# Moving low parts and differences of activation forms from VectorE to GpSimd in a one-layer decoder step

## The chip, the cores and the metric

The kernel runs on one core of a Trainium2 chip. In the profile the core's engines are PE (TensorE matmul), PEld (its weight load), DVE (VectorE), ACT (ScalarE), POOL (GpSimd) and SP (SyncE, here only a queue of transfers). The metric is the device time of one execution in microseconds (us). It is the median of three runs: 2129.26 us, with 2129.08 and 2132.24 as the lowest and the highest.

## The reference

One inference step of a hybrid decoder layer, in float32, for 512 prompt tokens and 8 sample tokens (so 520 columns of activations when features lie on the partitions):

```python
def trunk(x, ...):                       # DEPTH = 1, D_MODEL = 2048, D_FF = 5632
    m, c_new, s_new = mixer(rmsnorm(x, norm_mix_g), ...)
    x = x + m
    f, f_new = conv_ffn(rmsnorm(x, norm_ffn_g), ...)
    x = x + f
    return rmsnorm(x, final_norm_g), ...

def mixer(xn, ...):
    bg, cg, hin, q, k, v, og, glr = split(xn @ w_in, ...)       # 2048 x 6160
    ya = bg * causal_dwconv(cg * hin, conv_prev, conv_w)        # 1024 channels
    o, s_new = gla_chunked(q, k, v, logf, s0)                   # 4 heads
    yb = rmsnorm_per_head(o) * silu(og)
    return concatenate([ya, yb]) @ w_out, ...                   # 2048 x 2048

def conv_ffn(xn, ...):
    u, v = split(xn @ w_up, 2)                                  # 2048 x 11264
    return (silu(causal_dwconv(u, ...) + conv_b) * v) @ w_down  # 5632 x 2048
```

The outputs are the two sets of activations and the new convolution and recurrence states.

## The kernel before

**Number form.** Every float32 operand of a large product is held as two fp32r tiles, a high part `hi` (a rounding copy, made by ACT) and a low part `lo` = source - `hi` (made by DVE). A product is three matmul passes: high weights by high activations, low by high, high by low. For activations the function `split` makes the pair: line 123 is ACT's copy, line 124 is DVE's subtraction. For weights it is `prepare`: line 1381 (ACT) and line 1385 (DVE), on tiles of 128x1024.

**Seven products in place of eight.** From the second part of the input projection on, the products are done in a seven-product block scheme: the activations of a block row are combined into seven *forms* (numbers 1 to 7; 1, 2 and 3 are plain quarters, 4 to 7 are differences and sums), the weights into seven sums, and `ORDER = (1, 5, 6, 2, 7, 3, 4)` is the order in which the seven products are run. The table `INPUT = {1: 1, 2: 2, 3: 3, 4: 7, 5: 5, 6: 4, 7: 6}` says which form product r reads. Each product is 24 matmuls of 260 columns. A form exists for four groups of feature rows (g = 0 to 3), each a pair of 128x520 tiles.

**Stages.** Input projection with the recurrence; the *mixer* (12 sets of seven products, the rest of the input projection); the output projection (`wo`, two chunks of four groups, seven products each); the up projection of the ConvFFN (44 sets of seven); the down projection; the final norm. A loop over all products (the order's step i) emits, for each step, the matmuls, the evacuations of the step before (`mix_finish`, `chunk_finish` with DVE line 1670, `up_finish`), the parts of the weights for step i + 2 (`prepare`), and small steps of generators that say at which offset from their start they want to go on (`yield 7.5`). The program order that results is kept as it stands on PE, DVE, ACT, POOL and SP: each of them works strictly in that order.

**Where the output projection ends.** In its second chunk, the results of group g are complete after the group. The generator `projected(g)` (line 1693) then stores them (`x1_d`, SP), scales the four quarters into temporaries `xg[0..3]` (ACT, line 1707), makes the squares for the norm (ACT, added into `ssq` and `R` by POOL transfers, line 1717) and builds the forms of the up projection: forms 1, 2, 3 by `split`; t1, t2, t3, t4 by DVE (lines 702 and 696) for forms 5, 4, 6 and 7. Form 7 and, for the last group, all forms are split at once; t1, t2, t3 of the groups 0 to 2 go to memory (`t_d`, SP) and come back with `load_sum` in the last group, where `split_sums` splits them, each at a fixed offset. The up projection's first products read all of this. Forms 2 and 3 are written into the tiles of finished sums (`acc`), so that the writer must wait until the transfer to `x1_d` has read those.

**Where the mixer begins.** `load_sum(mt_d, f, g)` loads forms 5, 4, 6 and 7 of the layer's input, which were put in memory earlier; the lists `put[:3]`, `put[3:6]` and the generator `put_sums` split them at fixed places. Two of them (form 7, groups 0 and 1) use `split_by_dma`: ACT writes the high part and its negative, and a POOL transfer adds the source to that.

**Temporaries** come from a pool of eight 128x520 tiles that are used in turn.

Of the kernel before, what the change touches and what calls it, by code (L numbers as in the profile page):

```python
# [9 lines left out]
F32 = mybir.dt.float32  # L10
F32R = mybir.dt.float32r
U8 = mybir.dt.uint8
AF = mybir.ActivationFunctionType
ALU = mybir.AluOpType
# [8 lines left out]
T = NP + NS  # L23
# [14 lines left out]
def trunk_kernel(  # L38
# [6 lines left out]
    nc = tc.nc  # L45
# [46 lines left out]
    def tmp():  # L92
        return tp.tile([P, T], F32, tag="t", name="t")

    def two(ap):
        return ap.rearrange("p (a b) -> p a b", a=2)
# [24 lines left out]
    def split(src, hi, lo, scale=None):  # L121
        if scale is None:
            nc.scalar.activation(hi, src, AF.Copy)  # L123
            nc.vector.tensor_tensor(lo, src, hi.bitcast(F32), op=ALU.subtract)  # L124
        else:
            nc.scalar.activation(hi, src, AF.Copy, scale=scale)
            nc.vector.scalar_tensor_tensor(
                lo, src, scale, hi.bitcast(F32), op0=ALU.mult, op1=ALU.subtract
            )

    def split_by_dma(src, hi, lo, again=None):
        nc.scalar.activation(hi, src, AF.Copy)
        nc.scalar.activation(lo, hi.bitcast(F32), AF.Copy, scale=-1.0)
        again = src if again is None else again
        nc.gpsimd.dma_start(lo.bitcast(F32), again, accum_op=ALU.add)

    def halves(t):
        return t[:, :HT], t[:, HT:T]
# [115 lines left out]
    def moving(pool, tag, name):  # L254

        return pool.tile([P, T + 3], F32R, tag=tag, name=name)[:, 3:]

    def pair_tiles(pool, tag):

        return [  # L260
            moving(pool, f"{tag[0]}{s}{tag[1:]}", tag[0] + s) for s in "hl"
        ]
# [17 lines left out]
    t_d = dp.tile([3, 3, P, T], F32, name="t_d")  # L280
    mt_d = dp.tile([4, 4, P, T], F32, name="mt_d")
# [55 lines left out]
    with ExitStack() as es:  # L337
# [208 lines left out]
        for k in range(KD):  # L546
            c, t = k // 4, k % 4
# [147 lines left out]
    def minus(out, ps, x):  # L695
        nc.vector.scalar_tensor_tensor(out, ps, -1.0, x, op0=ALU.mult, op1=ALU.subtract)

    def add(out, x, y):
        nc.vector.tensor_tensor(out, x, y, op=ALU.add)  # L699

    def sub(out, x, y):
        nc.vector.tensor_tensor(out, x, y, op=ALU.subtract)
# [42 lines left out]
    def acc_tag(n):  # L745
        return f"x{'hl'[n % 2]}{8 + n // 2}"
# [5 lines left out]
    def form(f, g):  # L752

        if f == 1:
            x = pair_tiles(bigA, f"b{g}")
        elif f in (2, 3):
            x = [
                moving(bigA, acc_tag(4 * g + q), "b2")
                for q in ((0, 3) if f == 2 else (1, 2))
            ]  # L760
        else:
            k = homes.get((f, g), {5: 0, 4: 4, 6: 8, 7: 12}[f] + g)
            x = [moving(slots[k], f"y{s}{k}", f"y{s}{k}") for s in "hl"]
        for j, q in enumerate(zip(*(halves(y) for y in x))):
            xq[f, 2 * g + j] = q
        return x

    def first_tile(kind, g, m):

        return 4 * g + 2 * m if kind == "down" else 2 * g + 8 * m  # L770

    def rows_of(d, kind, g, q):

        m, b = first_tile(kind, g, q // 2), q % 2
        return d[m : m + 2, :, b * HT : (b + 1) * HT].rearrange("m p c -> p m c")
# [45 lines left out]
    def mix_source(n, m, k):  # L821
        what, j = MIX[n]
        c0 = {"ch": 1024 * m + j * P, "b": (j + m - 1) * P, "og": 5120 + (j + m - 1) * P}[what]
        return w_in[(k - 1) * 1024 : k * 1024, c0 : c0 + P].rearrange("(k p) c -> p k c", p=P)

    def second_half(source):

        raw = {}
        for k in (1, 2):
            w = raw[2, k] = wxr.tile([P, 1024], F32, tag="raw", name="raw")  # L830
            src = source(2, k)
            nc.sync.dma_start(w.rearrange("p (k c) -> p k c", k=src.shape[1]), src)
        return raw
# [11 lines left out]
    with ExitStack() as mix:  # L845
# [46 lines left out]
        with ExitStack() as gl:  # L892
# [9 lines left out]
            for j in range(4):  # L902
                nc.gpsimd.affine_select(
                    out=sel, in_=sel, compare_op=ALU.not_equal, fill=1.0,
# [340 lines left out]
            for h in range(NH):  # L1245
# [21 lines left out]
                for d in range(2):  # L1267
                    ps = group(h > 0 and d == 0)
                    t = gp.tile([P, T], F32, tag="v", name="v", bufs=2)
# [16 lines left out]
    NG = KD // 4  # L1286
# [19 lines left out]
    def raw_tile(source, k):  # L1306

        w, src = wp.tile([P, 1024], F32, tag="raw", name="raw"), source(1, k)
        return w, (w.rearrange("p (k c) -> p k c", k=src.shape[1]), src)
# [285 lines left out]
    def fh():  # L1595
        return wxp.tile([P, T], F32, tag="fh", name="fh")
# [94 lines left out]
    ssq, loaded = [], deque()  # L1691

    def projected(g):

        xg = {}

        def ready(q):
            a, m = acc[g, q], first_tile("wo", g, q // 2)
            kept = a
            if g == NG - 1 and q in (1, 2):  # L1700

                kept = tmp()[:, :T]
                nc.scalar.activation(kept, a, AF.Copy)
            nc.sync.dma_start(rows_of(x1_d, "wo", g, q), two(kept))
            xg[q] = tmp()[:, :T]
            for j in range(2):
                nc.scalar.activation(
                    halves(xg[q])[j], halves(a)[j], AF.Copy, scale=gffn[:, m + j : m + j + 1]
                )

        def square(q):
            if g == 0 and q in (0, 3):
                nc.scalar.activation(ssq[q % 2], acc[g, q], AF.Square)
                return
            sq = fh()
            nc.scalar.activation(sq, acc[g, q], AF.Square)
            nc.gpsimd.dma_start(ssq[q % 2], sq, accum_op=ALU.add)

        def out(f, t):

            if f == 7 or g == NG - 1:
                split(t, *form(f, g))
            else:
                nc.sync.dma_start(t_d[f - 4, g], t)

        yield 4.5
        ready(0)
        split(xg[0], *form(1, g))
        yield 5.5
        ready(3)  # L1730
        square(0)
        yield 6.5
        ready(1)
        square(3)
        yield 7
        t1, t2 = xg[0], tmp()[:, :T]
        sub(t1, xg[0], xg[1])
        minus(t2, t1, xg[3])
        yield 7.5
        ready(2)  # L1740
        out(5, t1)
        yield 8
        split(xg[2], *form(2, g))
        t4 = xg[2]
        minus(t4, t2, xg[2])
        yield 8.5
        out(4, t2)
        yield 9
        square(1)
        out(7, t4)  # L1750
        yield 10
        t3 = xg[1]
        sub(t3, xg[3], xg[1])
        yield 10.5
        square(2)
        out(6, t3)
        yield 11
        split(xg[3], *form(3, g))

    def load_sum(d, f, g, by_dma=False):  # L1760

        hi, lo = form(f, g)
        x = lo.bitcast(F32)
        nc.sync.dma_start(x, d[f - 4, g])
        if by_dma:
            return lambda: split_by_dma(x, hi, lo, d[f - 4, g])
        return lambda: split(x, hi, lo)

    def split_sums():

# [36 lines left out]
    wxr = yctx.enter_context(tc.tile_pool(name="raw2", bufs=4, side="right"))  # L1807
    wxp = yctx.enter_context(tc.tile_pool(name="sums", bufs=2, side="right"))
    early = second_half(lambda m, k: mix_source(0, m, k))
    put = [load_sum(mt_d, 5, g) for g in range(1, 4)]  # L1810
    early[1, 1], first = raw_tile(lambda m, k: mix_source(0, m, k), 1)
    nc.sync.dma_start(*first)
    ps = new_mm()
# [8 lines left out]
    assert not side  # L1822
    begin(0)
    load_rest(0)
    put += [load_sum(mt_d, 4, g) for g in range(1, 4)]
    on = [tmp()[:, :T] for _ in range(2)]
    for j, x in enumerate(on):
        nc.sync.dma_start(x, o_d[j])
    put += [load_sum(mt_d, 6, g) for g in range(1, 4)]
    y8, y9 = zpad[0][:, 2 : 2 + T], tmp()[:, :T]  # L1830
    evac(ps, y8)
    nc.scalar.activation(y8, y8, AF.Silu)
# [16 lines left out]
    bctx.close()  # L1849
    yt3 = yctx.enter_context(tc.tile_pool(name="yt3", bufs=1))  # L1850
    slots[12:] = [yt3] * 4
    put += [load_sum(mt_d, 7, g, g < 2) for g in range(4)]
    for k in range(8):
        for f, kk, b in ((1, k, 0), (2, k + 8, 0), (3, k + 8, 1)):
            xq[f, k] = [xa[kk][x][b] for x in range(2)]
# [7 lines left out]
        yield from leave(8, y8, y9)  # L1863

    def put_sums():
        for x, n in zip(put[6:], (1, 1.5, 2, 2.5, 3, 4, 4.5)):
            yield n
            x()

# [2 lines left out]
    for i, (kind, at, r) in enumerate(order):  # L1872
        j, n = i % 7, i // 7
# [41 lines left out]
        if i in (0, 2, NW, NW + 2):  # L1915

            x = xq[1, 0][0]
# [14 lines left out]
        if kind == "wo":  # L1932
            c, g = at
            if c == 0 and g == 2 and j == 0:
                load_form("wo", 1, 0)
            if c == 0 and j == 4 and g + 1 < NG:
                load_residual(g + 1)
            if c == 0 and g == 2 and j == 1:
                add_residual("wo", 0)
            if c == 0 and g == NG - 1 and j >= 1:  # L1940
                load_form("wo", 1, j)
            if c == 1 and g == NG - 1:

                for f, h in {
                    0: ((5, 0), (5, 1)), 2: ((5, 2),), 3: ((4, 0), (4, 1)), 4: ((4, 2),),
                    5: ((6, 0), (6, 1)), 6: ((6, 2),),
                }.get(j, ()):
                    loaded.append(load_sum(t_d, f, h))
        if 7 * n in (NM - 7, NU - 7):
            for x in {1: (0, 1), 2: (2, 3), 4: (4, 5), 6: (6,)}.get(j, ()):  # L1950
                load_form(groups[n + 1][0], 0, x)
# [2 lines left out]
        if kind == "down":  # L1954
            c, g = at
# [166 lines left out]
```

## Time and profile before

| What | Value |
|---|---|
| median of three runs | 2129.26 us |
| the profiled execution, its own time | 2130.32 us |
| span in its trace | 2128.6 us |
| PE busy | 2106.9 us (99%) |
| DVE busy | 1763.2 us (83%) |
| ACT busy | 1125.9 us (53%) |
| POOL busy | 421.0 us (20%) |
| granted TensorE clock, mean | 0.998 |

The profile lists, for each engine, when an instruction began, how long it took, and in square brackets how long the engine had been idle and what ended that. `x3` after a row means three like instructions in a row that are shown as one. Matmuls overlap: 24 matmuls of 260 columns are one product and follow each other in 2.86 us. DVE instructions overlap a little too: the start-to-start distance is smaller than the duration shown. "PE mm" and "PE ms" are products of the mixer and the up projection, "PE x", "y", "e" and "f" those of the output and the down projection, by the names of the accumulators.

### The profile page before, as it was taken

The page shows a single profiled execution, that of the slowest core. Times are in us where ns is not written, and L with a number is a line of the kernel's source. Part 1 is how long each engine was busy: PE and PEld are TensorE (multiplying, and loading weights), DVE is VectorE, ACT ScalarE, POOL GpSimd, SP SyncE. Part 2 cuts the span into 40 slices and gives each one's busy share as a digit, 9 for nine tenths or more (in the row PEclk, how much of TensorE's full clock was granted, in tenths as well). Part 3 has the DMA queues.
Part 4 walks back from the last instruction along what each step waited for, and adds up shares of the span by engine and source line. Part 5 has one row for each costly group of instructions (what it writes and reads, how often), then busy time and mean ns, then how long its engine had stood idle before and what let it go on. Part 6 is the DMA issues. An engine that isn't in the chain of part 4 may idle for free.

```text
span 2128.6 us, 44249 instructions
## 1 busy us (share of the span) xinstructions
PE 2106.9 (99%) x17880; PEld 2086.8 (98%) x17880; DVE 1763.2 (83%) x2355; ACT 1125.9 (53%) x1701; POOL 421.0 (20%) x614
## 2 busy tenths in 40 slices
PE   9999999999999989999999999999999999999997
PEld 8999999999999989999999999999999999999997
DVE  6566675988888998989889989989989778888886
ACT  7454554655544776555555555555555554444445
POOL 4211221121235211211311221212212200300000
PEclk9999999999999999999999999999999999999999
DMA  8456546877789995766766766766767876994734
GB/s 258 131 169 185 164 137 186 236 199 200 192 263 278 269 287 133 196 175 171 195 177 167 196 176 167 196 176 168 195 176 193 282 227 153 274 295 131 220 110 160
DMA packets 468190, 418.37 MB, mean 197 GB/s; under 512 B 21817, under 2 KB 426569, under 8 KB 467841
## 3 DMA queue, kind: packets, MB, share of 16 engines
q1 hardware_dynamic: 424209, 289.84, 48.0%
q0 software_dynamic: 43728, 125.63, 22.6%
q8 instruction: 140, 2.29, 0.5%
q14 instruction: 65, 0.53, 0.1%
q10 hardware_dynamic: 48, 0.07, 0.0%
HBM read 300.18 MB, written 80.31 MB: 179 GB/s over the span
## 4 chain that ended last, share of the span: by engine, by line
PE 93%; DVE 2%; DMA 2%; ACT 1%; issue 1%; POOL 0%; SPq 0%; ACTq 0%; DVEq 0%; POOLq 0%
PE mm L1408 37%; PE ms L1408 15%; PE mm L146 12%; PE x L1651 9%; PE y L1651 9%; PE e L1651 4%; PE f L1651 4%; DMA raw<-in_w_in_dram 1%; DMA wgraw<-in_w_in_dram 1%; PE ms L1071 0%; DMA yl<-t_d 0%; DVE yl L124 0%; DMA t_d<-t 0%; PE ms L2012 0%; PE tp L365 0%
## 5 line engine op out<-in xcount | busy, mean ns | idle before, releaser
L1408 PE MATMUL mm<-yh,hi 128*128 128x260 f32 x1792 | 500.8, 281 | 2.5 <-DVE t L699 1.3
L1408 PE MATMUL mm<-yl,hi 128*128 128x260 f32 x1792 | 498.9, 281 | 2.5 <-DVE yl L124 2.5
L1408 PE MATMUL mm<-yh,lo 128*128 128x260 f32 x1792 | 496.4, 280 | 0.0
L1381 ACT ACTIVATE hi<-raw 128x1024 fp32r<-128x1024 f32 x336 | 354.4, 1055 | 243.4 <-issue 89.0
L1385 DVE TENSOR_TENSOR lo<-raw,hi 128x1024 fp32r<-128x1024 f32 x336 | 410.3, 1221 | 45.3 <-ACT hi L1381 41.4
L1385 DVE TENSOR_TENSOR lo<-s,hi 128x1024 fp32r<-128x1024 f32 x252 | 309.3, 1228 | 132.7 <-ACT hi L1381 132.7
L1381 ACT ACTIVATE hi<-s 128x1024 fp32r<-128x1024 f32 x252 | 266.3, 1057 | 227.5 <-PE ms L1408 97.3
L1408 PEld LDWEIGHTS mm<-yh,hi 128*128 128x128 f32 x1792 | 337.7, 188 | 3.6 <-issue 1.5
L1408 PEld LDWEIGHTS mm<-yl,hi 128*128 128x128 f32 x1792 | 335.0, 188 | 3.3 <-DVE yl L124 3.3
L1408 PEld LDWEIGHTS mm<-yh,lo 128*128 128x128 f32 x1792 | 335.9, 189 | 0.0
L1408 PE MATMUL ms<-b,hi 128*128 128x260 f32 x1408 | 264.9, 280 | 0.0
L1408 PEld LDWEIGHTS ms<-b,hi 128*128 128x128 f32 x1408 | 222.0, 188 | 0.0
L1651 PE MATMUL y<-form,hi 128*128 128x260 f32 x1120 | 211.5, 281 | 0.8 <-DVE acc L1670 0.8
L1651 PE MATMUL x<-form,hi 128*128 128x260 f32 x1120 | 211.6, 281 | 0.0
L1326 DVE TENSOR_TENSOR s<-s,raw 128x1024 f32<-128x1024 f32 x168 | 205.3, 1222 | 2.9
L1408 PE MATMUL ms<-b,lo 128*128 128x260 f32 x704 | 196.4, 280 | 0.0
L1651 PEld LDWEIGHTS y<-form,hi 128*128 128x128 f32 x1120 | 176.5, 188 | 1.2 <-ACT yh L123 1.0
L1651 PEld LDWEIGHTS x<-form,hi 128*128 128x128 f32 x1120 | 176.5, 188 | 0.2
L1651 PE MATMUL x<-form,lo 128*128 128x260 f32 x560 | 156.9, 280 | 0.0
L1651 PE MATMUL y<-form,lo 128*128 128x260 f32 x560 | 156.8, 280 | 0.0
L1408 PEld LDWEIGHTS ms<-b,lo 128*128 128x128 f32 x704 | 132.0, 187 | 0.0
L1408 PE MATMUL mm<-bh,hi 128*128 128x260 f32 x448 | 124.9, 280 | 1.0 <-DVE acc L1670 1.0
(405 smaller groups left out, 4825.2 us busy)
## 6 DMA issues: line engine op xcount, KB each, us to landing
raw<-in_w_up_dram SPq DMA_DIRECT2D x176, 512.0 KB, 4.0
raw<-in_w_down_dram SPq DMA_DIRECT2D x96, 512.0 KB, 7.3
raw<-in_w_in_dram SPq DMA_DIRECT2D x92, 512.0 KB, 4.1
form<-f_d SPq DMA_DIRECT2D x126, 260.0 KB, 6.3
raw<-raw POOLq DMA_DIRECT2D x60, 512.0 KB, 5.8
f_d<-t POOLq DMA_DIRECT2D x80, 260.0 KB, 5.5
raw<-in_w_out_dram SPq DMA_DIRECT2D x32, 512.0 KB, 12.5
form<-g_d POOLq DMA_DIRECT2D x42, 260.0 KB, 7.5
```

The lines of the kernel that those rows point to most:

```text
L146: nc.tensor.matmul(o, w, xx, start=first and i == 0, stop=last and i == 2)
L1326: return lambda: nc.vector.tensor_tensor(out, x, y, op=ALU.add)
L1381: nc.scalar.activation(his[i], src, AF.Copy)
L1385: nc.vector.tensor_tensor(los[i], src, his[i].bitcast(F32), op=ALU.subtract)
L1408: nc.tensor.matmul(st["bank"][b], w[:, k, :], x, start=b not in st["used"] and (k, j) == (0, 0), stop=(k, j) == (7, 2), skip_group_check=True,
L1651: nc.tensor.matmul(ps[:, m, :], w[:, k, m * P : (m + 1) * P], x, start=b not in st["used"] and k == 0 and j == 0, stop=k == 3 and j == 2, ...
```

## The change

`split_by_pool` takes the place of `split_by_dma`: ACT makes the high part as before, and the low part is made by a GpSimd subtraction. It is used

- in `projected(g)` for groups 0 to 2 in forms 1, 2 and 3, and for all four groups in form 7;
- in `split_sums` for four of the nine loaded sums: form 5 of groups 0 and 1, form 4 of group 0, form 6 of group 0;
- where the mixer begins for forms 5, 4 and 6 of group 1 and form 7 of groups 0 and 2; form 7 of group 1 becomes a plain `split` (DVE), and two of the offsets of `put_sums` move by half a step.

The difference t3 of groups 0 to 2 goes to GpSimd as well (`psub`). In `projected(g)` form 2 is made 1.5 steps later (offset 9.5, behind forms 4 and 7) for all groups, and t4 gets a temporary of its own instead of being written over `xg[2]`.

```diff
-    def split_by_dma(src, hi, lo, again=None):
+    def split_by_pool(src, hi, lo):
         nc.scalar.activation(hi, src, AF.Copy)
-        nc.scalar.activation(lo, hi.bitcast(F32), AF.Copy, scale=-1.0)
-        again = src if again is None else again
-        nc.gpsimd.dma_start(lo.bitcast(F32), again, accum_op=ALU.add)
+        nc.gpsimd.tensor_tensor(lo, src, hi.bitcast(F32), op=ALU.subtract)
...
+    def psub(out, x, y):
+        nc.gpsimd.tensor_tensor(out, x, y, op=ALU.subtract)
...
     def projected(g):
-        xg = {}
+        xg, final = {}, g == NG - 1
+        some = split if final else split_by_pool
...
         def out(f, t):
-            if f == 7 or g == NG - 1:
+            if f == 7:
+                split_by_pool(t, *form(f, g))
+            elif final:
                 split(t, *form(f, g))
             else:
                 nc.sync.dma_start(t_d[f - 4, g], t)
...
-        split(xg[0], *form(1, g))
+        some(xg[0], *form(1, g))
...
         yield 8
-        split(xg[2], *form(2, g))
-        t4 = xg[2]
+        t4 = tmp()[:, :T]
         minus(t4, t2, xg[2])
...
         out(7, t4)
+        yield 9.5
+        some(xg[2], *form(2, g))
         yield 10
         t3 = xg[1]
-        sub(t3, xg[3], xg[1])
+        (sub if final else psub)(t3, xg[3], xg[1])
...
-        split(xg[3], *form(3, g))
+        some(xg[3], *form(3, g))
...
-    put = [load_sum(mt_d, 5, g) for g in range(1, 4)]
+    put = [load_sum(mt_d, 5, g, g == 1) for g in range(1, 4)]
...
-    put += [load_sum(mt_d, 7, g, g < 2) for g in range(4)]
+    put += [load_sum(mt_d, 7, g, g % 2 == 0) for g in range(4)]
...
-        for x, n in zip(put[6:], (1, 1.5, 2, 2.5, 3, 4, 4.5)):
+        for x, n in zip(put[6:], (1, 1.5, 2, 3, 3.5, 4, 4.5)):
...
-                    loaded.append(load_sum(t_d, f, h))
+                    loaded.append(load_sum(t_d, f, h, (f, h) in ((5, 0), (5, 1), (4, 0), (6, 0))))
```

POOL where the mixer begins (yl1, yl5 and yl9 are the low parts of forms 5, 4 and 6 of group 1; yl12, yl13, yl14 those of form 7 of groups 0, 1 and 2; `raw` is a weight sum that a transfer adds up; g_d is memory for the output projection's forms). Before:

```order
L1330 DMA raw_4540<-raw_4553 128x1024
L135 DMA yl12_4830<-mt_d_122 128x520
L135 DMA yl13_4833<-mt_d_122 128x520
L743 DMA g_d0_119<-fh_5031 128x260
```

And now:

```order
L1331 DMA raw_4540<-raw_4553 128x1024
L133 TENSOR_TENSOR yl1_4545<-yl1_4545,yh1_4544 128x520
L133 TENSOR_TENSOR yl5_4675<-yl5_4675,yh5_4674 128x520
L133 TENSOR_TENSOR yl9_4688<-yl9_4688,yh9_4687 128x520
L133 TENSOR_TENSOR yl12_4830<-yl12_4830,yh12_4829 128x520
L133 TENSOR_TENSOR yl14_4836<-yl14_4836,yh14_4835 128x520
L744 DMA g_d0_119<-fh_5029 128x260
```

Two transfers became five subtractions; DVE has lost yl1, yl5, yl9 and yl14 and gained yl13.

POOL at the end of the output projection, from group 2's forms to the norm's Newton step (b2 are forms 2 and 3, t_9654 is t3, yl14 and yl15 form 5 of groups 0 and 1, yl4 and yl8 forms 4 and 6 of group 0, yl1 form 7 of group 3). Before:

```order
L1717 DMA R_128<-fh_9774 128x520
L1717 DMA ssq_8908<-fh_9822 128x520
L1330 DMA raw_9664<-raw_9661 128x1024
L1717 DMA ssq_8908<-fh_9913 128x520
L1717 DMA R_128<-fh_9960 128x520
L1717 DMA R_128<-fh_10106 128x520
L1717 DMA ssq_8908<-fh_10157 128x520
```

And now:

```order
L133 TENSOR_TENSOR b2_9784<-t_9702,b2_9783 128x520
L700 TENSOR_TENSOR t_9654<-t_9617,t_9654 128x520
L1719 DMA ssq_8906<-fh_9823 128x520
L133 TENSOR_TENSOR b2_9859<-t_9617,b2_9858 128x520
L133 TENSOR_TENSOR yl14_9707<-yl14_9707,yh14_9706 128x520
L1331 DMA raw_9664<-raw_9661 128x1024
L1719 DMA ssq_8906<-fh_9914 128x520
L133 TENSOR_TENSOR yl15_9710<-yl15_9710,yh15_9709 128x520
L1719 DMA R_128<-fh_9961 128x520
L133 TENSOR_TENSOR yl4_9828<-yl4_9828,yh4_9827 128x520
L133 TENSOR_TENSOR yl1_10108<-t_10065,yh1_10107 128x520
L133 TENSOR_TENSOR yl8_9920<-yl8_9920,yh8_9919 128x520
```

The transfers of the norm's squares now stand between subtractions on POOL.

DVE for group 3, where the up projection has begun (yl3 and yl7 are forms 5 and 4 of group 3, b2 is its form 2, yl4, yl5 and yl6 form 4 of groups 0 to 2, yl1 and yl8 as above). Before:

```order
L124 TENSOR_TENSOR yl4_9827<-yl4_9827,yh4_9826 128x520
L1385 TENSOR_TENSOR lo_10023<-s_9660,hi_10021 128x1024
L124 TENSOR_TENSOR yl3_10032<-t_9866,yh3_10031 128x520
L124 TENSOR_TENSOR yl5_9830<-yl5_9830,yh5_9829 128x520
L124 TENSOR_TENSOR b2_10065<-t_10028,b2_10064 128x520
L696 SCALAR_TENSOR_TENSOR t_10028<-t_10010,t_10028 128x520
L124 TENSOR_TENSOR yl6_9874<-yl6_9874,yh6_9873 128x520
L1385 TENSOR_TENSOR lo_10073<-raw_9663,hi_10071 128x1024
L124 TENSOR_TENSOR yl7_10076<-t_10010,yh7_10075 128x520
L124 TENSOR_TENSOR yl1_10110<-t_10028,yh1_10109 128x520
L124 TENSOR_TENSOR yl8_9919<-yl8_9919,yh8_9918 128x520
```

And now:

```order
L1386 TENSOR_TENSOR lo_10024<-s_9660,hi_10022 128x1024
L124 TENSOR_TENSOR yl3_10033<-t_9867,yh3_10032 128x520
L124 TENSOR_TENSOR yl5_9831<-yl5_9831,yh5_9830 128x520
L694 SCALAR_TENSOR_TENSOR t_10065<-t_10011,t_10029 128x520
L124 TENSOR_TENSOR yl6_9875<-yl6_9875,yh6_9874 128x520
L1386 TENSOR_TENSOR lo_10071<-raw_9663,hi_10069 128x1024
L124 TENSOR_TENSOR yl7_10074<-t_10011,yh7_10073 128x520
L1327 TENSOR_TENSOR s_9660<-s_9660,raw_9663 128x1024
L1386 TENSOR_TENSOR lo_10118<-raw_9664,hi_10115 128x1024
L124 TENSOR_TENSOR b2_10121<-t_10029,b2_10120 128x520
```

Three low parts have left the stretch, and form 2 stands behind two more weight instructions.

More of the change, by code (lines that the diff above doesn't have):

```diff
@@ L1757, in projected, with load_sum @@
         yield 11
-        split(xg[3], *form(3, g))
-    def load_sum(d, f, g, by_dma=False):
+        some(xg[3], *form(3, g))
+    def load_sum(d, f, g, by_pool=False):
         hi, lo = form(f, g)
@@ L1764, in load_sum @@
         nc.sync.dma_start(x, d[f - 4, g])
-        if by_dma:
-            return lambda: split_by_dma(x, hi, lo, d[f - 4, g])
-        return lambda: split(x, hi, lo)
+        return lambda: (split_by_pool if by_pool else split)(x, hi, lo)
     def split_sums():
@@ L1824, in trunk_kernel @@
     load_rest(0)
-    put += [load_sum(mt_d, 4, g) for g in range(1, 4)]
+    put += [load_sum(mt_d, 4, g, g == 1) for g in range(1, 4)]
     on = [tmp()[:, :T] for _ in range(2)]
@@ L1828, in trunk_kernel @@
         nc.sync.dma_start(x, o_d[j])
-    put += [load_sum(mt_d, 6, g) for g in range(1, 4)]
+    put += [load_sum(mt_d, 6, g, g == 1) for g in range(1, 4)]
     y8, y9 = zpad[0][:, 2 : 2 + T], tmp()[:, :T]
```

## The prediction

> **What bounds the kernel now.** I read the page's busy times first, then what PE (TensorE) waits for, summed by releaser:
>
> ```profile
> PE 2106.9 (99%) x17880; PEld 2086.8 (98%) x17880; DVE 1763.2 (83%) x2355; ACT 1125.9 (53%) x1701; POOL 421.0 (20%) x614
> ...
> PE mm L1408 <- DVE yl L124: 2.5, 4, 1.2
> PE mm L1408 <- DVE t L699: 1.3, 1, 1.3
> ...
> PE mm L1408 <- DVE acc L1670: 1.0, 1, 1.0
> PE y L1651 <- DVE acc L1670: 0.8, 1, 0.8
> PE ms L1919 <- DVE acc L1670: 0.7, 1, 0.7
> PE mm L1408 <- ACT yh L123: 0.6, 2, 0.3
> PE mm L1408 <- ACT ms L1418: 0.5, 1, 0.5
> ```
>
> (Columns: total us, times, longest.) PE is busy 99%, so the change can win only these waits. They lie at two places: 0.5 and 1.3 where the mixer begins, and 2.5, 1.0, 0.8, 0.7 and 0.6, that is 5.6, between output and up projection (the *seam*). The window view of four stretches says who is full there; its columns are window, length, busy us (instructions) of PE, PEld, DVE, ACT, POOL, then clock, DMA share, GB/s:
>
> ```profile
> 364.00:390.00 26.00, 24.16 (x200) 23.77 (x199) 23.00 (x32) 19.08 (x31) 4.15 (x6) 1.00 1.10 307
> 707.83:728.13 20.30, 20.30 (x173) 20.30 (x172) 20.20 (x26) 16.08 (x26) 2.65 (x3) 1.00 0.91 244
> 728.13:748.42 20.29, 20.29 (x170) 20.11 (x170) 20.19 (x25) 16.07 (x26) 4.31 (x5) 1.00 0.96 252
> 769.66:798.36 28.70, 23.03 (x173) 21.22 (x174) 26.84 (x36) 22.52 (x39) 4.31 (x5) 1.00 1.11 300
> ```
>
> The second and third rows are groups 0 and 1 of the last output-projection chunk. DVE (VectorE) is busy 20.20 of 20.30 us there, and POOL (GpSimd) hardly at all. The chain of waits gives PE's own pace:
>
> ```profile
> 703.34 2.86 PE x L1651 x24
> ...
> 723.34 2.86 PE y L1651 x24
> ...
> 743.63 2.86 PE x L1651 x24
> ...
> 763.25 9.24 DMA t_d<-t
> 772.57 9.59 DMA yl<-t_d
> ```
>
> Seven products of 24 matmuls took 20.00 us (703.34 to 723.34), and in the next group 20.29. So DVE slows PE by 0.29 a group, although no wait is listed. At the seam two transfers follow each other in the chain, and the change leaves both where they are.
>
> **The price of a subtraction on either engine.** From the groups by form, and the timeline where DVE is gapless:
>
> ```profile
> L296 POOL TENSOR_TENSOR kc<-bc 128x512 f32<-128x512 f32 x4 | 4.6, 1147 | 10.5 <-DVE L L996 10.5
> L1385 DVE TENSOR_TENSOR lo<-s,hi 128x1024 fp32r<-128x1024 f32 x252 | 309.3, 1228 | 132.7 <-ACT hi L1381 132.7
> 745.45 0.69 DVE L1670 TENSOR_TENSOR acc<-acc,e 128x520 f32<-128x520 f32 x1
> 746.06 0.69 DVE L124 TENSOR_TENSOR b<-t,b 128x520 fp32r<-128x520 f32 x1
> 746.67 1.22 DVE L1385 TENSOR_TENSOR lo<-raw,hi 128x1024 fp32r<-128x1024 f32 x1
> ```
>
> A low part of 128x520 holds DVE for 0.61 us (746.06 to 746.67). On POOL the nearest shape, 128x512, took 1.15. What a POOL subtraction does to DVE beside it shows in the norm's Newton step, the one place with long POOL operations on these shapes:
>
> ```profile
> 813.37 1.31 POOL L300 TENSOR_TENSOR t<-t 128x520 f32<-128x520 f32 x1
> ...
> 816.33 2.17 POOL L302 TENSOR_TENSOR R<-R,t 128x520 f32<-128x520 f32 x1
> ...
> 813.44 2.33 DVE L1385 TENSOR_TENSOR lo<-s,hi 128x1024 fp32r<-128x1024 f32 x1 [1.97 <-ACT hi L1381]
> ...
> 817.42 0.43 DVE L699 TENSOR_TENSOR t<-mm,t 128x260 f32<-128x260 f32 x1
> ```
>
> The DVE low part at 813.44 has two operands in SBUF. It took 2.33 instead of 1.23, so 1.10 us of it went to the POOL operation that had begun at 813.37. The DVE operation at 817.42 reads a PSUM accumulator (`mm`), runs within POOL's 816.33 to 818.50, and took its usual 0.43. I therefore count a POOL subtraction as 1.0 us of DVE time if DVE's next operation has both operands in SBUF (1.15 less a late start, at most 1.10); 0.4 if one that reads PSUM is next (1.0 less its 0.61, as 745.45 to 746.06); and 0 if DVE idles. So a moved instruction can cost DVE more than the 0.61 that it saves.
>
> [...]
>
> **Part A, where the mixer begins.** Four low parts leave DVE and one comes, so it saves 3 x 0.61 = 1.83. Five come to POOL.
>
> ```profile
> 379.37 0.64 ACT L133 ACTIVATE yl<-yh 128x520 fp32r<-128x520 f32 x1
> ...
> 382.49 1.22 DVE L1385 TENSOR_TENSOR lo<-s,hi 128x1024 fp32r<-128x1024 f32 x1 [0.81 <-ACT hi L1381]
> ...
> 387.81 0.42 DVE L699 TENSOR_TENSOR t<-mm,t 128x260 f32<-128x260 f32 x1
> ...
> 388.38 0.36 PE L1408 MATMUL mm<-yh,hi 128*128 128x260 f32 x1 [1.33 <-DVE t L699]
> ```
>
> PE's 1.33 ends with DVE's evacuation at 387.81. DVE had one idle time ahead of it, 0.81, for a rounding copy by ACT (ScalarE). ACT loses two negations of 0.64, so this idle time goes. For the blocks I take three in full and two ahead of PSUM readers: 3 x 1.0 + 2 x 0.4 = 3.8. Together -1.83 + 3.8 - 0.8 = **+1.2**. Bounds: -1.8 (both PE waits vanish) and 5 x 1.10 - 1.83 = +3.7.
>
> **Part B, groups 0 to 2.** Five DVE instructions per group go to POOL: the low parts of forms 1, 2, 3 and 7, and t3. This saves 5 x 0.61 = 3.05. In the order, an accumulation from PSUM (line 1670) stands behind about half of the places where ACT's copy releases POOL, and for one I count nothing. So 2 x 1.0 + 2 x 0.4 = 2.8 come back, and DVE needs 20.29 - 3.05 + 2.8 = 20.04 against PE's 20.00. Almost the whole 0.29 is won in some 2.5 groups: **-0.6**. Bounds: 3 x -0.29 = -0.9, and 3 x (5 x 1.10 - 3.05) = +7.4 if every block counts in full.
>
> **Part C, the seam.**
>
> ```profile
> 767.30 0.70 DVE L124 TENSOR_TENSOR b<-t,b 128x520 fp32r<-128x520 f32 x1 [0.85 <-DMA x_d<-acc]
> ...
> 784.23 0.70 DVE L124 TENSOR_TENSOR b<-t,b 128x520 fp32r<-128x520 f32 x1 [1.59 <-DMA x_d<-acc]
> ...
> 786.19 1.22 DVE L1385 TENSOR_TENSOR lo<-raw,hi 128x1024 fp32r<-128x1024 f32 x1
> 787.33 1.30 DVE L124 TENSOR_TENSOR yl<-t,yh 128x520 fp32r<-128x520 f32 x2
> ...
> 783.68 0.62 ACT L123 ACTIVATE yh<-t 128x520 fp32r<-128x520 f32 x1
> ...
> 786.33 0.51 PE L1408 MATMUL mm<-yl,hi 128*128 128x260 f32 x2 [0.76 <-DVE yl L124]
> 788.08 0.51 PE L1408 MATMUL mm<-yl,hi 128*128 128x260 f32 x2 [1.24 <-DVE yl L124]
> ...
> 772.40 0.86 POOL L1330 DMA_DIRECT2D raw<-raw  x1 [7.25 <-DMA ssq<-fh]
> ```
>
> DVE waited 1.59 for the store of `acc` at form 2 of group 3 (784.23). Queued behind it were form 4's low part (the first of the two at 787.33), for which PE waited 1.24 at 788.08, and the weight's low part at 786.19. With form 2 behind, form 4's low part can start when ACT's copy ends, 783.68 + 0.62 = 784.30, so 3.0 us earlier. PE's waits on `yl` and `yh`, 2.5 + 0.6, are just that long. Six subtractions here now run on POOL (form 3 of group 2, four loaded sums, form 7 of group 3). Those before 782 us push DVE into the time of its old 1.59 wait, and cost nothing. I count one block in full near 785 and one at half: +1.6. Form 2 of group 3 itself comes three DVE instructions later; POOL's low parts of form 7 and of form 6, group 0, are released meanwhile, each 1.15 instead of 0.61: +0.4 for what PE may have to wait for one of them. The 0.85 at 767.30 becomes a wait on POOL, with the transfers of squares behind it, which only the norm needs, and that comes later. Sum -3.0 + 1.6 + 0.4 = **-1.0**. Bounds: all waits of the seam, -5.6, and 6 x (1.10 - 0.61) = +2.9.
>
> **Sum.** +1.2 - 0.6 - 1.0 = -0.4 against the profiled execution's 2130.32 us (span 2128.6 and 1.7 around it). That execution is 1.06 over the median of the three runs, so the forecast is 2129.26 - 0.4 = **2128.9**: no change.
>
> **The rivals.**
>
> *Slower: POOL's lock is paid in full in groups 0 to 2.* Its price is +7.4 less DVE's 0.1 of idle time in each of three groups, so +7.1. With A and C as forecast that is +7.3, so 2136.6. It decides from the point where the blocks of a group exceed the 3.05 saved. For it: DVE has no more than those 0.1 to take them in, and POOL starts right behind ACT's copy, when DVE is in the middle of weight instructions with two SBUF operands. Against it: about a quarter of DVE's instructions there are PSUM readers, and POOL too must wait until a running DVE instruction ends.
>
> *Faster: POOL finds the gaps.* If POOL's operations fall beside PSUM readers and idle time, A is -1.0, B -0.9, and C the whole -3.0: -4.9, so 2124.4. For it: the seam's stretch has DVE busy 26.84 of 28.70, and ACT loses work at the mixer. Against it: the two full stretches above, and that the low part at 813.44 met the very first POOL operation beside it.
>
> *POOL's queue is late.* POOL works in order, and its transfer at 772.40 stood 7.25 us in wait for `ssq`. A loaded sum's low part now stands near such transfers. If one is held by an issue (0.86) and another subtraction (1.15), C goes from -1.0 to +1.0: 2130.9. Against it: form 6 is read by the fifth of the first seven products and form 7 by the last.
>
> **How the numbers follow.** Forecast 0.55, slower by the lock 0.15, faster by the gaps 0.22, POOL's queue 0.08. What a measurement of this kernel can tell from no change is about 0.2%, 4.3 us. The forecast's own range is 2126 to 2132 (each of the three terms off by about 1), and the third rival's result lies in it. The range reaches to the results of the two outer rivals: **2123.5 to 2135.5**, which leaves out what of the faster one goes beyond it and most of the slower one, some 0.2 together. Faster by over 0.2% (below 2125.0) is the second rival, 0.22. Slower (above 2133.5) is the first, with 0.03 of mishaps of A and C at their upper bounds: 0.18. Within: 0.60.
>
> **What would show it.** Group distances in the chain near 20.04 instead of 20.29 show B right; above 20.29 the lock has won. DVE low parts of 128x1024 at 2.2 to 2.3 us beside POOL's show the lock, and their count its price. A is right if PE's wait on line 699 near 388 grows by about a microsecond; C if DVE's wait of 1.59 is gone and form 4's low part starts before 786. The forecast is wrong if POOL's subtraction takes much over 1.15 on these tiles, or if PE comes to wait on POOL.

## The result, and the profile after

The change makes the kernel slower: 2145.82 us (median of six runs, 2143.06 to 2147.72) against 2130.61, ratio 1.0070 with a 95% interval of 1.0057 to 1.0083. That is 15.2 us above before and 10 above the range given. The profiled execution has a span of 2144.2 us. Its page and what PE waits for (total us, times, longest):

```profile
PE 2113.5 (99%) x17880; PEld 2093.4 (98%) x17880; DVE 1778.2 (83%) x2332; ACT 1124.1 (52%) x1699; POOL 454.9 (21%) x637
...
PE f L1652 <- DVE lo L1386: 5.0, 3, 3.0
PE ms L1922 <- DVE acc L1671: 3.7, 1, 3.7
PE mm L1409 <- DVE t L697: 2.9, 1, 2.9
...
PE y L1652 <- DVE lo L1386: 1.6, 1, 1.6
```

DVE runs 23 instructions fewer and is busy 15 us longer. PE's waits for line 124's low parts of forms have shrunk from 2.5 us to 1.0. In their place PE waits 6.6 us for low parts of *weights*, which were on time before, and its waits for `acc` have grown from 2.5 to 4.7.

Both executions run the same 17,880 matmuls in the same order, so the delay can be read at the start of equal matmuls:

| place (time in the trace of before) | behind by, us | part of the prediction | forecast | measured |
|---|---|---|---|---|
| 379.4, in the mixer's beginning | -0.2 | | | |
| 394.3, behind it | +3.3 | A | +1.2 | about +3.3 |
| 720.8, before group 0's forms | +3.3 | | | |
| 727.5 / 747.8 / 768.1, groups 0, 1, 2 | +6.4 / +11.4 / +14.1 | B | -0.6 | +10.8 |
| 796.4, behind the seam | +15.5 | C | -1.0 | +1.4 |
| the end | +15.6 | | | |

Where the largest part goes, the timeline of the changed kernel shows (start us, duration us, and in brackets the idle time ahead and what ended it). DVE in groups 0 to 2, then POOL and PE in group 1:

```profile
721.88 5.31 DVE L1327 TENSOR_TENSOR s<-s,raw 128x1024 f32<-128x1024 f32 x1
...
735.82 2.33 DVE L1386 TENSOR_TENSOR lo<-raw,hi 128x1024 fp32r<-128x1024 f32 x1
...
749.45 7.14 DVE L1386 TENSOR_TENSOR lo<-s,hi 128x1024 fp32r<-128x1024 f32 x1
756.52 0.68 DVE L1671 TENSOR_TENSOR acc<-acc,e 128x520 f32<-128x520 f32 x1
...
775.45 5.26 DVE L1386 TENSOR_TENSOR lo<-s,hi 128x1024 fp32r<-128x1024 f32 x1 [0.85 <-ACT hi L1382]
...
748.68 0.85 POOL L1719 DMA_DIRECT2D R<-fh  x1 [7.25 <-ACT f L1677]
749.24 1.62 POOL L133 TENSOR_TENSOR yl<-t,yh 128x520 fp32r<-128x520 f32 x1
750.51 1.60 POOL L133 TENSOR_TENSOR b<-t,b 128x520 fp32r<-128x520 f32 x1
751.79 1.58 POOL L700 TENSOR_TENSOR t<-t 128x520 f32<-128x520 f32 x1
753.05 1.14 POOL L1719 DMA_DIRECT2D ssq<-fh  x1
753.66 1.84 POOL L133 TENSOR_TENSOR b<-t,b 128x520 fp32r<-128x520 f32 x1
...
756.65 0.59 PE L1652 MATMUL f<-form,lo 128*128 128x260 f32 x1 [2.99 <-DVE lo L1386]
```

One DVE instruction that takes 1.22 us alone lasts 7.14, from the first of four POOL subtractions to 1.1 us behind the end of the last (755.50). POOL starts one each 1.27 us while each lasts 1.6, so they overlap, and DVE does not get in between them; not even at the transfer issue in the row (753.05) did it. Group 0's three in a row cost 5.31 - 1.22 = 4.1, group 2's four cost 4.0 (5.26 at 775.45; DVE began 2.2 us into that run), group 1's 5.9. The four ran one behind the other because POOL's queue had been held for 7.25 us at the transfer ahead of them (748.68), while ACT made their high parts.

The second loss is the granted clock. The window view of three places (length, busy us and instructions of PE, PEld, DVE, ACT, POOL, then clock, DMA share, GB/s):

```profile
386.00:390.00 4.00, 1.28 (x11) 1.07 (x9) 3.97 (x9) 1.21 (x2) 1.28 (x3) 1.00 0.42 118
390.00:394.00 4.00, 3.81 (x20) 3.84 (x21) 3.96 (x6) 1.06 (x1) 0.87 (x1) 0.59 0.92 223
749.00:756.00 7.00, 4.66 (x40) 4.45 (x38) 7.00 (x2) 2.53 (x4) 6.50 (x6) 1.00 1.10 336
756.00:763.00 7.00, 6.35 (x30) 6.35 (x31) 6.92 (x7) 4.79 (x8) 3.98 (x3) 0.51 0.45 119
790.00:795.00 5.00, 1.34 (x10) 1.13 (x9) 4.97 (x5) 2.28 (x4) 2.19 (x2) 0.85 1.04 224
795.00:800.00 5.00, 5.00 (x25) 5.00 (x25) 4.90 (x8) 4.40 (x9) 0.00 (x0) 0.50 1.15 275
```

At the end of each of PE's three waits of about 3 us (2.92, 2.99, 3.66), or just behind it, the clock is halved, once for 3.4 us and twice for 6.8. The profiled execution of the kernel before has no such stretch there. The bound for what this costs is (3.4 + 6.8 + 6.8) / 2 = 8.5 us. The delay at equal matmuls gives less: it grows by 1.5, 2.7 and 1.7 us while the clock is halved, 5.9 together, and PE's busy time grew by 6.6 for the same matmuls. In groups 0 to 2, then, 8.1 of the 10.8 us were lost in waits at the full clock, 6.9 of them ahead of the first matmul at half clock. Nor does the loss need many such stretches: the two executions of the changed kernel with the highest mean clock, 0.997 against 0.994 in the profiled one, took 2143.06 and 2146.07.

### The profile page after: what moved, and what is told of

Read it like the earlier page. It is cut to its first block, busy times and chain, and to the rows that moved or that the text cites. A ratio compares the mean times of both kernels' runs of the same rounds, so it can differ in the third digit from the quotient of the medians.

```text
span 2144.2 us, 44267 instructions
## 1 busy us (share of the span) xinstructions
PE 2113.5 (99%) x17880; PEld 2093.4 (98%) x17880; DVE 1778.2 (83%) x2332; ACT 1124.1 (52%) x1699; POOL 454.9 (21%) x637
## 3 DMA queue, kind: packets, MB, share of 16 engines
q0 software_dynamic: 43440, 125.09, 22.3%
## 4 chain that ended last, share of the span: by engine, by line
PE 89%; DVE 4%; DMA 2%; issue 2%; ACT 1%; POOL 0%; SPq 0%; ACTq 0%; DVEq 0%; POOLq 0%
PE mm L1409 36%; PE ms L1409 14%; PE mm L144 12%; PE x L1652 8%; PE y L1652 8%; PE f L1652 3%; PE e L1652 3%; DVE lo L1386 2%; DMA raw<-in_w_out_dram 1%; DMA raw<-in_w_in_dram 1%; DMA wgraw<-in_w_in_dram 1%; PE ms L1072 0%; DVE yl L124 0%; PE ms L2015 0%; DVE acc L1671 0%
## 5 line engine op out<-in xcount | busy, mean ns | idle before, releaser
L1386 DVE TENSOR_TENSOR lo<-s,hi 128x1024 fp32r<-128x1024 f32 x252 | 324.4, 1287 | 133.4 <-ACT hi L1382 133.4
L1327 DVE TENSOR_TENSOR s<-s,raw 128x1024 f32<-128x1024 f32 x168 | 211.4, 1258 | 2.9
```

Source lines behind the costliest of these rows:

```text
L1327: return lambda: nc.vector.tensor_tensor(out, x, y, op=ALU.add)
L1386: nc.vector.tensor_tensor(los[i], src, his[i].bitcast(F32), op=ALU.subtract)
```

## The experiments

**Theory.** POOL's subtractions keep a DVE instruction waiting for a whole *run* of them, as long as the next one is ready (5.31 and 7.14 us above, for three and four in place of 1.22); with PE's waits that follow, its clock is halved (three times above). What the two engines contend for is not shown by any run: the port of the expectations and the lock of the prediction are names for this waiting, whose first case was the 2.33 us at 813.44 in the kernel before. **Rivals:** each subtraction blocks singly for 1.1 us at most, as the prediction priced it, and the rest is order; or POOL's busy time as such, or its queue and the transfers in it, is what costs.

### One part at a time

The mixer's beginning alone (before, with the change's lines of `load_sum(mt_d, ...)` and `put_sums`):

```diff
-    put += [load_sum(mt_d, 7, g, g < 2) for g in range(4)]
+    put += [load_sum(mt_d, 7, g, g % 2 == 0) for g in range(4)]
```

> Only the part of the change where the mixer begins. In the changed kernel's trace PE has lost 3.3 us against before when that place is passed. If the parts are independent and the loss there is the blocks of single subtractions plus a half clock for 3.4 us: 2130.6 + 3.3 = 2133.9, with a wait of PE for line 697's t near 390 of about 2.9. If that loss came from what runs later, or varies from run to run: within 1 of 2130.6.

2133.58 us, ratio 1.0011 (1.0002 to 1.0021): +2.7, near the 3.3. All five subtractions are paid in full: five DVE instructions there are each 1.10 to 1.12 us too long, 5.5 together, in this kernel as in the changed one. PE's wait is again 2.9, and in this execution the half clock behind it lasted 6.8 us (3.4 in the changed kernel); it took 2136.08, more than the median:

```profile
391.00:399.00 8.00, 8.00 (x46) 8.00 (x47) 6.26 (x8) 3.45 (x5) 2.30 (x3) 0.64 0.73 168
```

The projection alone (the changed kernel, with the mixer's beginning of before and its `split_by_dma`):

```diff
-    put += [load_sum(mt_d, 7, g, g % 2 == 0) for g in range(4)]
+    put += [load_sum(mt_d, 7, g, by_dma=g < 2) for g in range(4)]
```

> Only the part in the output projection and its seam; the mixer's beginning as before. Theory 'held for the run': 15.2 - 3.3 = +12, so 2142.5, with VectorE instructions of 5 to 7 us beside runs of three and four subtractions, and two half-clock stretches of 6.8 us. Rival 'single blocks of 1.1': at most +7.4 + 2.9 of the prediction's bounds, so under 2141, and no VectorE instruction over 2.4.

2140.97, ratio 1.0053 (1.0033 to 1.0073): +10.1 where 12 were expected; only one half-clock stretch, of 3.4 us, was in the profiled execution, behind a wait of 3.34; another wait of 3.12 was followed by none. The time alone could still fit single blocks, which the expectation put under 2141. Its long DVE instructions, of 5.32, 7.50 and 4.49 us, do not. The longest:

```profile
747.17 7.50 DVE L1392 TENSOR_TENSOR lo<-s,hi 128x1024 fp32r<-128x1024 f32 x1
```

### The same places without reading

```diff
-        nc.gpsimd.tensor_tensor(lo, src, hi.bitcast(F32), op=ALU.subtract)
+        nc.gpsimd.memset(lo.bitcast(F32), 0.0)
```

(and likewise for t3).

> The changed kernel with every new GpSimd subtraction replaced by a fill of the same tile with zero (the low parts and t3 are left out of the result): the same places in POOL's queue, the same relief of VectorE, but no operand read. Theory of the shared port: no VectorE instruction there is over 1.5 us, no half clock, and the whole gain of the moved work shows: 2122 to 2127. Rival 'the loss comes from the order, from POOL's queue or from the transfers behind it': still 2138 to 2146.

2125.62, ratio 0.9973 (0.9962 to 0.9984). No DVE instruction in the three stretches is longer than in the kernel before, and the mixer's beginning has no wait left:

```profile
364.00:392.00 28.00, 28.00 (x237) 28.00 (x236) 25.91 (x35) 20.87 (x33) 6.82 (x11) 1.00 1.08 303
724.00:746.00 22.00, 22.00 (x187) 22.00 (x186) 19.10 (x22) 17.64 (x29) 6.92 (x11) 1.00 1.05 274
```

So the order and the transfers behind POOL's work are not the cause, and taking these instructions off DVE is worth 5 us; the subtractions on POOL turn that into a loss of 15. A fill is shorter, 0.53 us, than a subtraction, so the length of POOL's work was not held equal; the next experiment has fills in runs. Against the expectation, the third stretch, the seam, had a half clock of 3.4 us.

### Runs on dead tiles

In 17 sets of the up projection of the kernel before:

```diff
+            for _ in range(many):
+                nc.gpsimd.tensor_tensor(ssq[0], R, R, op=ALU.subtract)   # or memset, or tensor_scalar
```

> The kernel before, with extra GpSimd work on dead tiles in 17 sets of the up projection: runs of 1, 2, 3, 4 and 6 subtractions of 128x520 (each waits for the one ahead, since all write one tile), runs of four fills (no operand read) and of four operations with one operand. Theory 'held for the run': POOL keeps the port only while its next operation is ready at once; here each must wait for the one ahead, so VectorE gets in between, and its longest instruction beside a run is 2.2 to 2.6 us whatever the run's length; beside the fills it stays at 1.22. Rival 'POOL's busy time counts': VectorE's instruction lasts until the whole run is over, 1.2 + 1.3 n, so 3.8 us for two, 6.4 for four and 9 for six. Rival 'not the port but the POOL queue': no instruction of VectorE is above 1.5.

A run of six, each waiting for the one ahead; and a run of four fills, DVE and then POOL:

```profile
1419.79 2.35 DVE L1385 TENSOR_TENSOR lo<-raw,hi 128x1024 fp32r<-128x1024 f32 x1
1422.06 1.54 DVE L124 TENSOR_TENSOR t<-t 128x520 fp32r<-128x520 f32 x1
1423.53 0.42 DVE L699 TENSOR_TENSOR t<-mm,t 128x260 f32<-128x260 f32 x1
1423.87 1.73 DVE L1326 TENSOR_TENSOR s<-raw 128x1024 f32<-128x1024 f32 x1
1425.52 2.07 DVE L1385 TENSOR_TENSOR lo<-raw,hi 128x1024 fp32r<-128x1024 f32 x1
...
1419.98 9.72 POOL L1933 TENSOR_TENSOR ssq<-R 128x520 f32<-128x520 f32 x6
...
1180.40 0.69 DVE L124 TENSOR_TENSOR t<-t 128x520 fp32r<-128x520 f32 x1
1181.35 1.22 DVE L1326 TENSOR_TENSOR s<-raw 128x1024 f32<-128x1024 f32 x1
...
1180.38 2.32 POOL L1937 MEMSET ssq<- 128x520 f32 x4
```

The theory's forecast holds: where POOL must wait between its operations, the two engines take turns, and no DVE instruction is above 2.35 whatever the run's length. Beside fills DVE keeps its usual times, 0.69 and 1.22, and an instruction that reads PSUM (1423.53) keeps its 0.42. "POOL's busy time counts" falls: six subtractions did not make a DVE instruction of 9 us. "Not the port but the POOL queue" falls too, since 2.35 is above its 1.5. An operation of POOL with one operand costs little: 1.30 or 1.63 in place of 1.22 for 1024 columns, 1.11 in place of 0.69 for 520.

The one execution took 2138.77, and its trace shows something else. Up to 977 us it runs the kernel before unchanged, and in the seam PE's longest wait is 1.24, as in that kernel; yet from 787.05 the clock was halved for 6.8 us. A half-clock stretch in the seam therefore does not need a wait of 3 us.

### Runs of one, two and three in the kernel itself

```diff
+    MOVED = {0: (7,), 1: (7, 2), 2: (7, 2, 6), 3: (7,)}
...
-        some = split if final else split_by_pool
+        def some(f, *x):
+            (split_by_pool if f in MOVED[g] else split)(*x)
...
-        (sub if final else psub)(t3, xg[3], xg[1])
+        (psub if 6 in MOVED[g] else sub)(t3, xg[3], xg[1])
```

> The changed kernel, but of the group's five subtractions only a run of one (form 7, group 0), two (forms 7 and 2, group 1) and three (forms 7, 2 and t3, group 2) stay on POOL; the others are VectorE's again. Theory 'held for the run': the VectorE instruction that meets the run lasts 1.2 + 1.0 + 1.27 (n - 1), at most: 2.3, 3.6 and 4.9 us. Rival 'single blocks': at most 2.4 us in all three groups. The time is between before and the changed kernel: 2136 to 2142.

DVE and POOL for one subtraction (726) and three in a row (772 to 776):

```profile
726.14 2.79 DVE L1327 TENSOR_TENSOR s<-s,raw 128x1024 f32<-128x1024 f32 x1
...
773.21 4.29 DVE L1386 TENSOR_TENSOR lo<-s,hi 128x1024 fp32r<-128x1024 f32 x1
...
772.27 1.63 POOL L133 TENSOR_TENSOR yl<-t,yh 128x520 fp32r<-128x520 f32 x1
773.55 1.61 POOL L133 TENSOR_TENSOR b<-t,b 128x520 fp32r<-128x520 f32 x1
774.84 1.56 POOL L700 TENSOR_TENSOR t<-t 128x520 f32<-128x520 f32 x1
```

One costs 2.79 - 1.22 = 1.6, more than the 1.1 that I expected; three cost 3.1 though DVE began 0.9 into the run, and it ends 1.1 behind the run's end. The two of group 1 met no long DVE instruction (1.50 at most, 3.6 expected at most). The time of its one execution, 2146.1, was above the 2136 to 2142 expected. The trace shows a reason that no rival had named:

```profile
796.72 9.54 POOL L133 TENSOR_TENSOR yl<-t,yh 128x520 fp32r<-128x520 f32 x1
...
807.55 2.10 PE L1409 MATMUL mm<-yl,hi 128*128 128x260 f32 x8 [5.06 <-POOL yl L133]
```

Here it is the other way round: DVE had begun first and ran 11 instructions back to back until 805.1, and POOL's one subtraction, 1.6 us long elsewhere, lasted 9.54. PE waited 5.06 for it.

### A copy between two subtractions

```diff
         nc.gpsimd.tensor_tensor(lo, src, hi.bitcast(F32), op=ALU.subtract)
+        nc.gpsimd.tensor_copy(spot, lo.bitcast(F32)[:, :1])
```

(and likewise behind t3).

> The changed kernel with more work on POOL: behind every new subtraction a copy of one column of its result, which must wait until the subtraction has ended. The subtractions of a run then don't overlap any more. Theory 'held for the run': VectorE gets in between, as in the runs on dead tiles, no VectorE instruction is above 2.6 us there, and the kernel gets faster although POOL does more: groups 0 to 2 lose 4 to 7 us instead of 10.8, total 2136 to 2141. Rival 'each subtraction costs its own block, however they stand', or 'POOL is late': unchanged or slower, 2145 to 2150.

Half as expected. DVE gets in between: its longest instruction in groups 0 to 2 is 2.80, and what its instructions take above their usual time falls from 6.1, 7.0 and 5.1 us in the three groups to 4.3, 1.9 and 3.4. But the time rose, to 2154.01 (ratio 1.0110, 1.0094 to 1.0125), above even the 2145 to 2150 of the rivals. With the copies POOL's queue needs 13 to 15 us for a group's five, so the transfers of the squares behind them are late, and ACT, which works in order, waits for their buffer:

```profile
752.15 0.64 ACT L1721 ACTIVATE fh<-acc 128x520 f32<-128x520 f32 x1 [8.38 <-DMA ssq<-fh]
...
754.69 0.58 ACT L1680 ACTIVATE f<-x 128x520 f32<-128x520 f32 x1
```

PE waited 5.4 us for ACT's `f` at that place. So breaking up the rows made the rival of POOL's queue true, and this experiment does not show what the rows cost in time.

### Only subtractions that stand alone

```diff
-        some(xg[2], *form(2, g))
+        split(xg[2], *form(2, g))
...
-        (sub if final else psub)(t3, xg[3], xg[1])
+        sub(t3, xg[3], xg[1])
```

(and form 7 of groups 0 to 2 by `split`; forms 1 and 3 stay on POOL).

> The changed kernel, but in groups 0 to 2 only forms 1 and 3, which stand alone on POOL, are made there; forms 2, 7 and t3, which made the runs, are VectorE's. The rest (mixer's beginning, loaded sums, form 7 of the last group) as changed. Theory: each subtraction alone costs VectorE 1.1 to 1.6 and saves 0.61, so a group pays about 2 x 0.75 = 1.5 where the changed kernel pays 3.0 to 4.0, and no VectorE instruction there is above 2.8: groups 0 to 2 lose 3 to 5 instead of 10.8, total 2137 to 2141. Rival 'the runs have nothing to do with it, the loss is the relief that went wrong elsewhere (order, seam)': 2144 to 2147.

2137.10, ratio 1.0032 (1.0020 to 1.0044). This is the strongest evidence: with nine of the fifteen subtractions of groups 0 to 2 taken back, 8.7 us of the 15.2 return. At equal matmuls this execution is behind by 4.9 before group 0's forms and by 4.9 after group 2's: the six that stay cost nothing there, less even than the 3 to 5 expected. At that price nine more would cost little; in rows with others they cost 8.7. It lowers the number in a group from five to two along with the rows, though. Five a group, each alone and with nothing else made late, were not run. The rows of group 1, DVE and POOL:

```profile
750.65 2.21 DVE L1386 TENSOR_TENSOR lo<-raw,hi 128x1024 fp32r<-128x1024 f32 x1
752.79 0.68 DVE L1671 TENSOR_TENSOR acc<-acc,x 128x520 f32<-128x520 f32 x1
753.39 1.73 DVE L1327 TENSOR_TENSOR s<-raw 128x1024 f32<-128x1024 f32 x1
...
750.49 1.29 POOL L133 TENSOR_TENSOR b<-t,b 128x520 fp32r<-128x520 f32 x1 [1.72 <-DMA x_d<-acc]
752.49 1.54 POOL L133 TENSOR_TENSOR bl<-t,bh 128x520 fp32r<-128x520 f32 x1 [0.71 <-ACT bh L132]
```

Blocks of 0.99 and 0.51, the second shortened by the PSUM reader at 752.79: these are near the prices that the prediction used, 1.0 and 0.4.

### The order alone

Before, with form 2 behind forms 4 and 7, nothing on POOL:

```diff
-        split(xg[2], *form(2, g))
-        t4 = xg[2]
+        t4 = tmp()[:, :T]
...
         out(7, t4)
+        yield 9.5
+        split(xg[2], *form(2, g))
```

> The kernel before with only the order of the change: form 2 made 1.5 steps later, behind forms 4 and 7, t4 in a temporary of its own; nothing on POOL. The prediction's step on form 4's low part in group 3 says -3.0 from the 1.59 us wait for the store of acc that no longer stands ahead of it: 2127.5 to 2128.5, and the low part starts before 786 of the old count. If something else at the seam is late anyway: 2130 to 2131.

2131.60, ratio 1.0002 (0.9993 to 1.0011): no change. The step itself is there: form 4's low part starts at 785.03 in place of 787.33, and PE gains about 2 us by the matmul that stood at 788.7. Then it loses 1.3 of them again, part of it in a wait of 0.8 for form 2's own low part:

```profile
L1408 PE MATMUL ms<-b,hi 128*128 128x260 f32 x1408 | 265.3, 280 | 1.2 <-DVE b L124 0.8 <-ACT b L123 0.4
```

With form 2 between them (form 7 last):

```diff
         square(1)
+        split(xg[2], *form(2, g))
+        yield 9.5
         out(7, t4)
```

> The kernel before with form 2 made behind form 4 but ahead of form 7 (offset 9, form 7 at 9.5), nothing on POOL. In the kernel with form 2 last, form 4's low part came 2.3 us earlier and PE won 2.0, then lost 1.35 again in a wait for form 2's low part. If form 2 in between is early enough for its product, the 2.0 stays: 2128.5 to 2129.5, and no wait of PE for line 124's b. If form 4 or form 7 is held by it again: 2130 to 2131.5.

2130.92, ratio 1.0003 (0.9994 to 1.0012): no change either; the wait moved on. In its trace DVE idles 2.15 us for ACT's copy of form 2 at 789.25, and the gain is given back by 796.

### ScalarE and a transfer in POOL's place

```diff
-        some = split if final else split_by_pool
+        some = split if final else split_by_dma
```

(and for the loaded sums and the mixer's forms; t3 and the last form 7 on DVE).

> The changed kernel with the same low parts taken off VectorE, but made by ScalarE (the negative of the high part) and a POOL transfer that adds the source, so that POOL's compute does not touch the port; t3 and form 7 of the last group are VectorE's. Theory of the port: no VectorE instruction above 1.5 us, no half clock from a VectorE stall, and most of the -5.3 of the fills comes true unless ScalarE becomes the bound: ScalarE has 16.1 of 20.3 us busy per group and gets four negatives of 0.53 more, 18.2 of 20. Expected 2126 to 2130; if transfers or ScalarE's order are late, 2131 to 2140.

2151.31, ratio 1.0093 (1.0080 to 1.0107), far from the 2126 to 2130 and above the 2131 to 2140 of its alternative. PE's waits, and ACT, DVE and PE around the longest:

```profile
PE y L1658 <- DVE acc L1677: 6.6, 2, 6.4
PE mm L1415 <- DMA yl<-mt_d: 4.6, 2, 3.3
PE mm L1415 <- DMA yl<-t_d: 4.5, 2, 3.0
...
780.94 0.64 ACT L137 ACTIVATE b<-b 128x520 fp32r<-128x520 f32 x1 [5.84 <-DMA x_d<-acc]
...
782.55 1.23 DVE L1392 TENSOR_TENSOR lo<-raw,hi 128x1024 fp32r<-128x1024 f32 x1 [6.36 <-ACT hi L1388]
...
785.48 0.56 PE L1658 MATMUL y<-form,hi 128*128 128x260 f32 x1 [6.37 <-DVE acc L1677]
```

The added transfers land late. And ACT, which now makes the negatives, stood still for 5.84 us at one of them until a store was done; DVE waited behind it for a weight's rounding copy, and PE behind DVE. No DVE instruction in the groups took longer than usual, so blocks by POOL played no part; but this way of making low parts brings a loss of its own, and says nothing of what POOL's subtractions cost.

## Why the prediction was wrong

- **What bounds the kernel** was right: DVE is full in the groups, and every microsecond added to it there reaches PE. Of the 9.0 us that POOL's blocks added to DVE in groups 0 to 2 beyond what it was spared, 8.1 reached PE at the full clock. Relief of DVE is worth what the faster rival said in sum: -4.9 forecast for work that costs DVE nothing, -5.3 measured with fills. That agreement is in part luck: its parts A, B and C were -1.0, -0.9 and -3.0, and the fills gained 2.4, 0.6 and 2.4 there and lost 0.7 in between.
- **The price of one subtraction** was right for one alone: 1.10 to 1.12 five times in the mixer, 0.5 to 1.0 for isolated ones in groups. It was too low in a few places, with 1.6 to 1.7 (the 2.79 above; 2.95 at 729.47 in the changed kernel). A subtraction itself took POOL some 1.3 to 1.6 us, not 1.15.
- **Part B is the step that failed.** I counted five separate blocks, "2 x 1.0 + 2 x 0.4 = 2.8" a group, and gave as the worst case 5 x 1.10. Measured were 6.1, 7.0 and 5.1. I let each subtraction start right behind ACT's copy and gave a discount to those ahead of a PSUM reader. But POOL's order puts forms 7 and 2 and t3 next to each other, with form 3 behind one transfer issue. They ran as one row, which held a single DVE instruction from where it began to the end of the row, and no PSUM reader could shorten that. Five blocks at the full 1.10 would be 5.5, so most of the error is the discount, and the rest is that a row can cost more than that. The groups are 21.6 and 22.3 us apart at the first products of groups 0, 1 and 2, where I forecast 20.04. The slower rival had the right place and sign, but its "2136.6" was too low: 1.10 per block was no upper bound, and even my three upper bounds together, 3.7 + 7.4 + 2.9 = 14.0, lie under the 15.2.
- **Part A** was mis-sized. I took 3.8 for the five blocks, two of them short; all five were full, 5.5. PE's wait for the evacuation (line 699, now 697) grew from 1.33 to 2.92, and the half clock behind it added 1.5.
- **The clock** was no term of the sum at all. In the profiled execution the delay grew by 5.9 us under the half clock, of which 4.2 stand in parts A and B.
- **Part C**: the gain on form 4's low part was real, 2.3 us earlier for 3.0 forecast, but the order alone brings nothing in the end, since form 2 is late instead: about 1.3 for my +0.4. The blocks in the seam sum to 5.3 us for my 1.6 (one in full and one at half would be 1.5 by my own prices), and the third half-clock stretch lies there.
- **POOL's queue** (the third rival) did not cost what I gave it, a late low part. It did something else: it held the subtractions until several were ready, and so made the rows. A late low part from POOL (5.06 us) and late squares (5.4) appeared only in experiments.

What stays open: how much of the loss would remain if five subtractions a group stood apart, for no kernel here has that without another loss; what the half clock costs in the median rather than in one execution; and whether the two subtractions of the seam that DVE met (2.2 and 1.0) would be harmless if placed elsewhere.

## What to carry to other kernels

Work handed from a full VectorE to GpSimd was not free here. A GpSimd subtraction that stood alone beside VectorE instructions with both operands in SBUF kept VectorE waiting for 0.5 to 1.7 us, 1.10 to 1.12 five times in the mixer, where a low part taken off it spares 0.61; three or four in a row kept it for 4.0 to 5.9. So count, as an estimate from these, for each such subtraction its whole duration as VectorE time, and for a row of ready ones the whole row, and look in the order for rows. One alone, just ahead of an instruction that reads PSUM, may pay (0.51 at 753.39); several that a queue had gathered did not. And where a stall of TensorE nears 3 us, allow for a half clock with it or behind it; 16 of 17 such stalls here had one.

## What the runs showed of the hardware that I had not expected

- A run of overlapping GpSimd subtractions (one each 1.27 us, 1.6 long) kept a 1.22 us VectorE instruction waiting for 5.31 to 7.14 us, with a transfer issue inside the run. If each waits for the one ahead, the engines alternate (2.35 at most).
- The reverse holds too: VectorE's gapless instructions kept one GpSimd subtraction, elsewhere 1.6 long, for 9.54 us, until 1.1 behind the last of 11. The prediction's "POOL too must wait until a running DVE instruction ends" has one case in the kernel before: POOL's operation of 2.17 at 816.33 ended 1.18 behind DVE's low part, which ran from 815.93 to 817.32. With 11 instructions, as with a run of three or four subtractions, the wait went beyond one instruction.
- Fills of GpSimd (no operand read) left VectorE's times as they were (0.69 and 1.22 beside four of them); an operation with one operand, which reads SBUF too, cost it only about 0.1 to 0.4 us (1.30 and 1.63 in place of 1.22, 1.11 in place of 0.69).
- Of PE's 17 waits of 2.85 us or more in the traces of this case, 16 came with a half clock of 3.4 or 6.8 us that began in the wait or at most 1.4 us behind it. The other one is the 3.12 in the kernel with the projection alone. The mean clock of these seven executions is 0.993 to 0.997, against 0.998 in the kernel before. The same wait of 2.9 was followed by 3.4 in the changed kernel and by 6.8 with the mixer's part alone. In the kernel with fills one stretch of 3.4 us stood in the seam although no single wait there was above 1.4, and in the kernel with runs on dead tiles one of 6.8 although none was above 1.24.
